# Beginning the stores of normed rows on GpSimd instead of SyncE in a one-core transformer step

## The chip, the cores and the metric

The kernel runs on one core of one Trainium2 chip. Its time is the device time of one execution in microseconds (us), from a run of the whole program; of several runs the median is given. A profile is one further execution with the hardware profiler on. In it the core's engines are PE (TensorE: matmuls), DVE (VectorE), ACT (ScalarE), POOL (GpSimd) and SP (SyncE, which does no arithmetic and here only begins DMAs). Each engine works through its own queue in order, and an instruction that waits for a semaphore holds up whatever stands behind it in that queue.

## What is computed

One layer of a decoder, for a prompt of 2048 tokens and for 64 sampled tokens (8 sequences of 8 tokens with a paged cache of 8192 past positions each). Two groups of heads, one of forgetting attention and one of matrix memory (mLSTM), share an input projection and an output projection. What bears on the change is the block behind them:

```python
def _layer_norm(x, g, b):
    mu = jnp.mean(x, -1, keepdims=True)
    var = jnp.mean(jnp.square(x - mu), -1, keepdims=True)
    return (x - mu) * lax.rsqrt(var + LN_EPS) * g + b

def _block_out(x, fox_h, m_h, ...):
    mix = jnp.concatenate([fox_h, mn], axis=-1) @ w_o      # output projection, 1024 x 1024
    x1 = _layer_norm(DN_ALPHA * x + mix, ln1_g, ln1_b)
    hid = jnp.square(jax.nn.relu(x1 @ w1))                 # MLP, 1024 -> 4096 -> 1024
    return _layer_norm(DN_ALPHA * x1 + hid @ w2, ln2_g, ln2_b)
```

Everything is float32. A product of two float32 matrices is made of three matmuls on high and low halves (`mm3`: lines 157, 158 and 159), and the halves are split by ACT (`split_hi`, line 149) and DVE or GpSimd (`split_lo`, line 152).

## The kernel before, in words

The prompt's 2048 rows are 16 tiles of 128 rows. The kernel goes through stages: the input projection and the matrix memory, the prompt's attention, then the output projection (`phase_o`) and the MLP (`phase_c`). The attention of the sampled tokens runs beside all of them in small steps (`sample_attention`, paced by `tick`): each step gathers pieces of the paged cache by indirect DMAs that GpSimd begins (lines 1671 for keys, 1788 for values), transposes the keys on DVE (1677), and does small products on PE (1700, 1812, 1769) between those of the stage. It ends during the MLP.

**Output projection.** For each tile t, `mix` (SP, line 1299) loads the mixed heads into a landing tile `xr`, of which there are two, and splits them: the high half on ACT, the low half `ml` on GpSimd (L152). `begin` (SP, line 1328) loads the tile's input row into `y`, one of five row buffers that go round. `unit` makes 24 matmuls for each half of the columns and adds them to the row on DVE (1335). `end` norms the row and stores it to a scratch tensor `dx1` in HBM (line 1340). For tiles 2 to 13 the program says, in this order, mix of tile t+1, begin, both units, end; the first and last tiles are written out by hand.

**MLP.** The tiles go in four blocks of four, the last with the 64 sampled rows as a fifth. In a block, `hidden(fc)` and `output(fc)` alternate over 16 slices of the hidden width. Weights come by SP (line 1255) into four buffers `wr`, which the two vectors of the norm share (145), and are split by ACT and DVE. The first output of a block loads the rows `y` from `dx1` by ACT (line 1471), into the same five row buffers; later ones add to them on DVE (1489). Before the last output of a block, `load` brings the next block's rows in for PE (line 1272 on SP, line 1284 on PE). The last output norms each row and stores it to the result (line 1497). The last tile of all, tile 15, has a norm of its own (`last_norm`), which stores its two halves by SP and ACT (line 194).

**The norm** (`layer_norm`, lines 162 to 177) goes over four engines: DVE takes the statistics (170, 171, 172), GpSimd the power -1/2 (173), DVE a product (174), ACT applies scale and bias (175), DVE multiplies by g (176), and GpSimd adds b (177). The store that follows thus waits for GpSimd. In `last_norm` the power on GpSimd is line 188; DVE's last step, line 193, needs it.

**What sets the order.** A planner orders the instructions of each engine from the program's dependences before the program is built, so what stands in the source behind something need not stand there in the queue. The built program begins to differ between the two kernels with the first moved store. A buffer's next writer waits until all readers of the last content are done; for a row that was stored, until the store has landed. Every DMA that one engine's path begins counts on one of eight semaphores in turn, and waits for the one that used it before.

Of the kernel before, what the change touches and what calls it, by code (L numbers as in the profile page):

```python
# [52 lines left out]
def body(ctx, tc, I, O, stages):  # L53
    nc = tc.nc
    V, A, G, T, SY = nc.vector, nc.scalar, nc.gpsimd, nc.tensor, nc.sync
# [17 lines left out]
    dx1 = drm.tile([TOT, D], F32, name="dx1")  # L73
# [69 lines left out]
    def bcast(src, off, n, name, pool=cst, **kw):  # L143
        t = pool.tile([128, n], F32, name=name, **kw)
        SY.dma_start(t, dap(src, off, [[0, 128], [1, n]]))
        return t

    def split_hi(dst, src, scale=1.0):
        last["ACT"] = A.activation(dst, src, AF.Copy, scale=scale)  # L149

    def split_lo(dst, src, hi, eng=None):
        r = (eng or V).tensor_tensor(dst, src, hi.bitcast(F32), op=OP.subtract)  # L152
        if eng is None:
            last["DVE"] = r
# [1082 lines left out]
    def landing(n=128):  # L1237

        return pcw.tile([128, 1024], F32, name="xr", bufs=2)[:n]

    def half_wo(hf, q):

        r = raw().rearrange("p (k c) -> p k c", k=2)
        SY.dma_start(r, I["w_o"][0, q * 256:(q + 1) * 256, hf * 512:(hf + 1) * 512].rearrange("(k p) c -> p k c", p=128))
        return r
# [17 lines left out]
    def row():  # L1263
        return C["py"].tile([128, D], F32, name="y", bufs=5)
# [24 lines left out]
    def phase_o(halves):  # L1289
        C["py"] = es_c.enter_context(tc.tile_pool(name="py", bufs=1, side="right", reuse_waits="tile"))  # L1290
        C["pc"] = pc = es_c.enter_context(tc.tile_pool(name="pc", bufs=1, reuse_waits="tile"))
        es, es_b, es_x = ExitStack(), ExitStack(), ExitStack()
        po_ = es.enter_context(tc.tile_pool(name="po", bufs=1, reuse_waits="tile"))
        pob = es_b.enter_context(tc.tile_pool(name="pob", bufs=1, side="right", reuse_waits="tile"))
        ppo = es.enter_context(tc.tile_pool(name="ppo", bufs=1, space=PSUM, reuse_waits="tile"))

        def mix(t, eng):
            mr = landing().rearrange("p (k c) -> p k c", k=8)
            SY.dma_start(mr, dmv[:, :, t * 128:(t + 1) * 128])
            mh = po_.tile([128, 8, 128], F32R, name="mh", bufs=2)  # L1300
            ml = po_.tile([128, 8, 128], F32R, name="ml", bufs=2)
            split_hi(mh, mr)
            split_lo(ml, mr, mh, eng)
            return mh, ml

        vx["more"] = lambda: pob.tile([128, 1024], F32, name="vx", bufs=2)
        wh, wl = [[], []], [[], []]

        def weights(hf):
            for q in range(4):  # L1310
                r = halves.pop(0) if halves else half_wo(hf, q)
                if hf == 0:
                    h, l = piece(None, r)
                    if q == 0:
                        V.memset(pc.tile([128, 512], F32, name="hq", bufs=1)[:, 0:1], 0.0)
                else:
                    h = pob.tile([128, 2, 512], F32R, name="woh", bufs=4)
                    l = pob.tile([128, 2, 512], F32R, name="wol", bufs=4)
                    split_hi(h, r)
                    split_lo(l, r, h)  # L1320
                wh[hf] += [h[:, 0], h[:, 1]]
                wl[hf] += [l[:, 0], l[:, 1]]

        m, xs = {}, {}

        def begin(t):
            xs[t] = row()
            SY.dma_start(xs[t], x_of(t))

        def unit(t, hf):  # L1330
            s = slice(hf * 512, (hf + 1) * 512)
            ps = ppo.tile([128, 512], F32, name="pw", bufs=4)
            for k in range(8):
                mm3(ps, m[t][0][:, k], m[t][1][:, k], wh[hf][k], wl[hf][k], k == 0, k == 7)
            V.scalar_tensor_tensor(xs[t][:, s], xs[t][:, s], ALPHA, ps, op0=OP.mult, op1=OP.add)
            tick(5.1)

        def end(t):
            layer_norm(xs[t], 128, *gb, pc, "1")
            SY.dma_start(dx1[t * 128:(t + 1) * 128], xs[t])  # L1340

        m[0] = mix(0, None)
        weights(0)
        m[1] = mix(1, None)
        begin(0)
        begin(1)
        unit(0, 0)
        weights(1)
        unit(1, 0)
        gb = [bcast(I[f"ln1_{x}"], 0, D, f"{x}1", pcw, tag="wr", bufs=4) for x in "gb"]  # L1350
        unit(0, 1)
        m[2] = mix(2, G)
        end(0)
        unit(1, 1)
        end(1)
        for t in range(2, 14):
            if t == 13:
                vx["more"] = None
            m[t + 1] = mix(t + 1, G)
            begin(t)  # L1360
            unit(t, 0)
            unit(t, 1)
            end(t)

        m[15] = mix(15, G)
        begin(14)
        begin(15)
        nx = [x1_load(0), x1_load(1)]
        unit(14, 1)
        take_back()  # L1370
        unit(15, 1)
        es_b.close()
        C["px"] = es_c.enter_context(tc.tile_pool(name="px", bufs=1, side="right", reuse_waits="tile"))
        ppx = es_x.enter_context(tc.tile_pool(name="ppx", bufs=1, space=PSUM, side="right", reuse_waits="tile"))
        px_of = lambda: ppx.tile([128, 4, 128], F32, name="px", bufs=2)
        x1_turn(0, 0, nx[0], px_of)
        nx.append(x1_load(2))
        unit(14, 0)
        x1_turn(1, 1, nx[1], px_of)
        nx.append(x1_load(3))  # L1380
        end(14)
        unit(15, 0)
        x1_turn(2, 2, nx[2], px_of)
        x1_turn(3, 3, nx[3], px_of)
        C["w1"] = w1_pieces(0)
        end(15)
        es_x.close()
        es.close()


    def phase_c():
# [38 lines left out]
        for ci, blk in enumerate(CB):  # L1430
# [3 lines left out]
            ys = {}  # L1434
# [25 lines left out]
            def output(fcs):  # L1460
                w2p = [piece(w2[fc * 256 + k * 128:fc * 256 + k * 128 + 128].rearrange("(k p) c -> p k c", p=128)) for fc in fcs for k in range(2)]
                h = [x for fc in fcs for x in H.pop(fc)]
                if 15 in fcs:
                    gb = vecs(2)
                for t in (blk[-1:] + blk[:-1] if 15 in fcs and ci == 3 else blk):
                    n = tok_n(t)
                    s = slice(off[t], off[t] + n)
                    if 0 in fcs:
                        ys[t] = row()
                        with tc.issue_after(last["ACT"].ins):  # L1470
                            A.dma_start(ys[t][:n], dx1[tok_r(t):tok_r(t) + n])
                        if t == 16:
                            V.memset(ys[t][64:128], 0.0)
                    for hf in range(2):
                        cs = slice(hf * 512, (hf + 1) * 512)
                        ps = ppc.tile([128, 512], F32, name="py", bufs=3)
                        for k in range(len(h)):
                            wh, wl = (x[:, 0, cs] for x in w2p[k])
                            if t == 16:
                                mm2(ps, h[k][2], wh, wl, k == 0, k == len(h) - 1)  # L1480
                            else:
                                mm3(ps, h[k][0][:, s], h[k][1][:, s], wh, wl, k == 0, k == len(h) - 1)
                        y = ys[t][:, cs]
                        if 15 in fcs and t == 15 and hf == 1:
                            last_norm(ys[t], n, *gb, pc, ps, O["y_prompt"][0, t * 128:(t + 1) * 128])
                        elif 0 in fcs:
                            V.scalar_tensor_tensor(y, y, ALPHA, ps, op0=OP.mult, op1=OP.add)
                        else:
                            V.tensor_tensor(y, y, ps, op=OP.add)  # L1489
                        tick(1.28 * len(fcs))  # L1490
                    if 15 in fcs and t == 16:
                        lo = landing(64)
                        A.copy(lo, ys[t][64:128])
                        V.tensor_tensor(ys[t][:64], ys[t][:64], lo, op=OP.add)
                    if 15 in fcs and (t, ci) != (15, 3):
                        layer_norm(ys[t][:n], n, *gb, pc, "2")
                        SY.dma_start(O["y_sample"].rearrange("b t d -> (b t) d") if t == 16 else O["y_prompt"][0, t * 128:(t + 1) * 128], ys[t][:n])

            for fc in range(16):
                if fc == 14:  # L1500
# [436 lines left out]
```

## Time and profile before

| what | us |
|---|---|
| median of three runs | 3315.42 |
| lowest and highest run | 3301.81 and 3319.17 |
| the profiled execution | 3323.93 |
| its span, first to last instruction | 3322.2 |
| first and last store of L1340 begun | 1392.9 and 1588.4 |
| first and last store of L1497 begun | 2009.5 and 3312.5 |

A row of instructions in a timeline has the start in us, the time it took, the engine, the line of the kernel, the operation, and what it writes and reads. In brackets stands how long the engine was idle before it and what ended that. A line with groups has the count behind an x, then the busy time and the mean of one in ns, then the idle time before them by what ended it. A row of waits reads: engine and line, then the engine (or DMA) and line it waited for, total us, times, longest. SPq and ACTq are the queues' own instructions: for a DMA they show when it was begun, not when its data landed.

### The profile page before, as it was taken

What the parts mean: (1) busy time and instruction counts of PE and PEld (TensorE: products, weight loads), DVE (VectorE), ACT (ScalarE), POOL (GpSimd) and SP (SyncE); (2) the same over time, 40 slices, a digit from 0 to 9 for tenths busy, and PEclk for the clock granted to TensorE, in tenths of its full rate; (3) what the DMA queues carried; (4) which work ended last, traced back from release to release, by engine and by line L of the source; (5) the groups of instructions that cost most, each with busy time, mean ns of one, the idle gap of its engine ahead of it and who ended that gap; (6) DMA issues with size and microseconds to landing.
All of it is one profiled execution on the core that took longest, in us unless ns stands there. A gap on an engine that the chain in (4) does not pass through costs nothing. (4 is left out here: it accounts for less than half of the span.)

```text
span 3322.2 us, 57307 instructions
## 1 busy us (share of the span) xinstructions
PE 3208.5 (97%) x21420; PEld 2637.1 (79%) x21420; DVE 2121.7 (64%) x5161; ACT 1357.2 (41%) x2670; POOL 931.2 (28%) x1060
## 2 busy tenths in 40 slices
PE   9999999999999999899999999999999999999997
PEld 8998797787877777677777777777767777889997
DVE  6857667566577877556566667656676545755555
ACT  4444244344377777313332333232333333433332
POOL 0112122323254443475333224332242210100001
PEclk9999999999999999999999999999999999999999
DMA  5665766877642233787777678767677554532221
GB/s 172 167 191 177 224 211 190 283 238 226 211 123 86 77 88 108 251 292 254 271 263 259 239 246 304 260 224 273 215 266 258 198 181 142 165 124 86 87 82 67
DMA packets 427294, 646.22 MB, mean 195 GB/s; under 512 B 83149, under 2 KB 320017, under 8 KB 426121
## 3 DMA queue, kind: packets, MB, share of 16 engines
q1 hardware_dynamic: 350184, 363.09, 36.1%
q0 software_dynamic: 74304, 270.57, 22.3%
q10 hardware_dynamic: 2528, 8.91, 0.7%
q8 instruction: 169, 2.77, 0.3%
q14 instruction: 109, 0.89, 0.1%
HBM read 589.63 MB, written 52.83 MB: 193 GB/s over the span
## 5 line engine op out<-in xcount | busy, mean ns | idle before, releaser
L1677 DVE STREAM_TRANSPOSE kT<-kT 128x512 f32<-128x512 f32 x512 | 331.8, 686 | 273.1 <-DMA kT<-cache_k,idxK 272.4
L149 ACT ACTIVATE wh<-wr 128x1024 fp32r<-128x1024 f32 x268 | 278.6, 1056 | 517.7 <-PE py L159 295.1
L1489 DVE TENSOR_TENSOR y<-y,py 128x512 f32<-128x512 f32 x475 | 319.0, 679 | 245.0 <-PE py L159 230.4
L1671 POOL DMA_INDIRECT kT<-cache_k,idxK x256 | 267.3, 1044 | 715.1 <-PE sQ L1700 626.3
L157 PE MATMUL ph<-x1h,wh 128*128 128x512 f32 (+1 forms) x1280 | 455.9, 356 | 8.8 <-ACT wh L149 7.3
L159 PE MATMUL ph<-x1h,wl 128*128 128x512 f32 (+1 forms) x1280 | 452.4, 355 | 4.2 <-DVE wl L152 4.1
L158 PE MATMUL ph<-x1l,wh 128*128 128x512 f32 (+1 forms) x1280 | 453.7, 355 | 0.0
L157 PE MATMUL py<-wh,h 128*128 128x512 f32 x1024 | 402.7, 396 | 3.5 <-DVE y L1489 3.1
L152 DVE TENSOR_TENSOR wl<-wr,wh 128x1024 fp32r<-128x1024 f32 x268 | 333.4, 1249 | 106.1 <-PE ph L159 40.7
L159 PE MATMUL py<-wh,h 128*128 128x512 f32 x1024 | 401.2, 393 | 0.0
L158 PE MATMUL py<-wl,h 128*128 128x512 f32 x1024 | 401.1, 392 | 0.0
L157 PE MATMUL pm<-whi,xhT 128*128 128x256 f32 (+2 forms) x1040 | 302.7, 291 | 3.1 <-ACT acb L542 2.1
L158 PE MATMUL pm<-wlo,xhT 128*128 128x256 f32 (+2 forms) x1040 | 297.6, 286 | 0.0
L159 PE MATMUL pm<-whi,xlT 128*128 128x256 f32 (+2 forms) x1040 | 296.8, 285 | 0.7 <-DVE xlT L152 0.7
L157 PEld LDWEIGHTS ph<-x1h,wh 128*128 128x128 f32 x1280 | 242.2, 189 | 45.8 <-ACT wh L149 8.0
L159 PEld LDWEIGHTS ph<-x1h,wl 128*128 128x128 f32 x1280 | 242.3, 189 | 39.8 <-DVE wl L152 5.4
L158 PEld LDWEIGHTS ph<-x1l,wh 128*128 128x128 f32 x1280 | 242.5, 189 | 33.7 <-issue 2.0
L1788 POOL DMA_INDIRECT vt<-cache_v,idxV x156 | 162.8, 1044 | 316.1 <-PE sO L1812 261.5
L157 PEld LDWEIGHTS py<-wh,h 128*128 128x128 f32 x1024 | 192.4, 188 | 50.7 <-DVE y L1489 6.1
L159 PEld LDWEIGHTS py<-wh,h 128*128 128x128 f32 x1024 | 192.2, 188 | 42.7 <-issue 2.9
L158 PEld LDWEIGHTS py<-wl,h 128*128 128x128 f32 x1024 | 192.4, 188 | 39.9 <-issue 4.1
L157 PEld LDWEIGHTS pm<-whi,xhT 128*128 128x128 f32 (+1 forms) x1040 | 198.4, 191 | 10.4 <-issue 5.3
(420 smaller groups left out, 6623.0 us busy)
## 6 DMA issues: line engine op xcount, KB each, us to landing
wr<-w SPq DMA_DIRECT2D x256, 512.0 KB
wra<-w_in SPq DMA_DIRECT2D x112, 512.0 KB
Rb<-dR SPq DMA_DIRECT2D x128, 128.0 KB
wr<-w_o SPq DMA_DIRECT2D x16, 512.0 KB
xr<-dmix SPq DMA_DIRECT2D x16, 512.0 KB
y<-x_prompt SPq DMA_DIRECT2D x16, 512.0 KB
dx<-y SPq DMA_DIRECT2D x16, 512.0 KB
xr<-dx SPq DMA_DIRECT2D x16, 512.0 KB
```

Source lines behind the costliest of these rows:

```text
L149: last["ACT"] = A.activation(dst, src, AF.Copy, scale=scale)
L152: r = (eng or V).tensor_tensor(dst, src, hi.bitcast(F32), op=OP.subtract)
L157: T.matmul(ps, wh, xh, start=first, stop=False)
L158: T.matmul(ps, wh, xl, start=False, stop=False)
L159: last["PE"] = T.matmul(ps, wl, xh, start=False, stop=stop)
L1489: V.tensor_tensor(y, y, ps, op=OP.add)
L1671: G.indirect_dma_start(out=piece(n), out_offset=None, in_=ck, in_offset=IO(ap=idxK[:, b, j // 2, j % 2:j % 2 + 1], axis=0))
L1677: V.transpose(x, x)
L1788: vx["last"] = G.indirect_dma_start(out=vt.rearrange("p f c -> p (f c)"), out_offset=None, in_=cv, in_offset=IO(ap=idxV[:, b, (kt % 4) * 4 ...
```

## The change

Two lines: the stores that follow `layer_norm` in the output projection (16, one for each tile) and in the MLP (16: fifteen tiles of the prompt and the sampled rows) are begun on GpSimd's queue, where the norm's last sum runs, and no more on SP's.

```diff
         def end(t):
             layer_norm(xs[t], 128, *gb, pc, "1")
-            SY.dma_start(dx1[t * 128:(t + 1) * 128], xs[t])
+            G.dma_start(dx1[t * 128:(t + 1) * 128], xs[t])
...
                     if 15 in fcs and (t, ci) != (15, 3):
                         layer_norm(ys[t][:n], n, *gb, pc, "2")
-                        SY.dma_start(O["y_sample"].rearrange("b t d -> (b t) d") if t == 16 else O["y_prompt"][0, t * 128:(t + 1) * 128], ys[t][:n])
+                        G.dma_start(O["y_sample"].rearrange("b t d -> (b t) d") if t == 16 else O["y_prompt"][0, t * 128:(t + 1) * 128], ys[t][:n])
```

The sampled rows' first norm (`sampled`), which stores to `dx1` too, and `last_norm` stay as they were. The arithmetic is the same. The order in which the planner sets the instructions of all engines changes from the first moved store on: in GpSimd's queue 32 transfers come in, in SP's 32 go, and on PE, DVE and ACT the same instructions stand in a partly different order.

## The prediction, made before the changed kernel ran

> **What bounds the kernel now.** I read the page first, then the busy time by stretches, the waits of the queues, and the timelines around the stores that move.
>
> ```profile
> span 3322.2 us, 57307 instructions
> ...
> PE 3208.5 (97%) x21420; PEld 2637.1 (79%) x21420; DVE 2121.7 (64%) x5161; ACT 1357.2 (41%) x2670; POOL 931.2 (28%) x1060
> ```
>
> TensorE (PE) is busy for 97% of the span; what its idle time leaves is 3322.2 - 3208.5 = 114 us. The view of stretches shows how much of that lies where the moved stores are (first column the stretch, second its length, third PE busy; after the brackets of DVE and ACT comes POOL, which is GpSimd).
>
> ```profile
> core 0: us, PE busy (x) PEld busy (x) DVE busy (x) ACT busy (x) POOL busy (x), PEclk, DMA share, GB/s
> ...
> 1392.00:1540.00 148.00, 144.73 (x918) 112.26 (x916) 80.62 (x200) 34.30 (x57) 101.31 (x82) 1.00 0.82 285
> 1540.00:1590.00 50.00, 43.92 (x285) 33.01 (x284) 32.40 (x68) 15.26 (x24) 29.67 (x21) 0.90 0.74 245
> ...
> 1980.00:2060.00 80.00, 73.99 (x477) 56.11 (x476) 55.47 (x110) 25.71 (x37) 40.46 (x34) 0.98 0.83 296
> ...
> 2420.00:2500.00 80.00, 73.27 (x448) 55.72 (x441) 58.10 (x111) 30.46 (x44) 40.11 (x32) 0.98 0.80 289
> ...
> 2860.00:2940.00 80.00, 77.39 (x447) 68.39 (x446) 51.52 (x79) 34.22 (x56) 11.90 (x8) 0.98 0.52 165
> ...
> 3306.00:3322.00 16.00, 0.00 (x0) 0.00 (x0) 8.89 (x11) 0.37 (x1) 5.64 (x3) 0.57 0.24 98
> ```
>
> The first two rows are the output projection from its first store on, the next three the ends of MLP blocks 0, 1 and 2, the last the tail after the last matmul. PE idles in them, tail aside, for 3.27 + 6.08 + 6.01 + 6.73 + 2.61 = 24.7 us. That is all that a better fed PE could win near these stores. The tail has no PE at all: there every delay counts in full.
>
> **The change part by part.** *What leaves SyncE (SP).* 16 stores of L1340 and 16 of L1497 leave its queue. They stood there as waiters:
>
> ```profile
> SPq L1497 <- POOL y L177: 89.8, 10, 24.7
> ...
> SPq L1340 <- POOL y L177: 83.5, 15, 11.1
> ...
> SPq L1328 <- DMA dx<-y: 20.4, 9, 3.8
> ```
>
> For 89.8 + 83.5 = 173 us SP stood at a store whose sum (L177, on GpSimd) was not done, with loads behind it. This looks large, but 173 us of a queue's standing is no time of PE. What PE waited for says how much of it arrived:
>
> ```profile
> PE sO L1812 <- DMA vt<-cache_v,idxV: 10.2, 7, 2.2
> PE ph L157 <- ACT wh L149: 7.3, 2, 5.0
> PE sO L1812 <- DMA xr<-cache_v,idxV: 6.8, 5, 3.4
> PE px L1284 <- DMA xr<-dx: 4.9, 2, 2.6
> ```
>
> The first and third are gathers that GpSimd itself begins; the second lies at 2500 to 2860, away from the stores. Only the fourth hangs on an SP load near moved stores: two waits, 4.9 us, at the ends of blocks 0 and 1. In SP's order both loads stand ahead of that block's first store, so they win nothing:
>
> ```profile
> 1988.45 0.54 SPq L1272 DMA_DIRECT2D xr<-dx  x1
> 2009.53 0.36 SPq L1497 DMA_DIRECT2D y_prompt<-y  x1
> ...
> 2432.80 6.50 SPq L1272 DMA_DIRECT2D xr<-dx  x2
> 2455.98 0.34 SPq L1497 DMA_DIRECT2D y_prompt<-y  x1
> ```
>
> Bounds of this part: 0 and -24.7 us (all PE idleness above); I take -1 us, near the rows.
>
> *What GpSimd gets.* 32 starts of plain transfers, which this trace never shows on GpSimd. The nearest row is its own gather of as many bytes (512 KB, 128 rows of 4 KB), and against it SP's start of the same store:
>
> ```profile
> L1671 POOL DMA_INDIRECT kT<-cache_k,idxK x256: 932/946/2037, 184.7 to 2575.4; - x128
> ...
> DMA to landing us min/median/max: 4.2/8.2/16.3
> L1340 SPq DMA_DIRECT2D dx<-y x16: 319/326/729, 1392.9 to 1588.4; - x16
> ```
>
> A start is bounded by 0.32 us (if it costs no more than on SP) and 2.04 us (the slowest gather); I take the median, 0.95 us, plus 0.25 us, the gap ahead of a gather in GpSimd's rows below (5.2 us over 20): 1.2 us. 32 x 1.2 = 38 us of GpSimd. Its densest stretch is the projection:
>
> ```profile
> L177 POOL TENSOR_TENSOR y<-y,b 128x1024 f32<-128x1024 f32 x12 | 28.7, 2397 | 23.0 <-DVE y L176 23.0
> L152 POOL TENSOR_TENSOR ml<-xr,mh 128x1024 fp32r<-128x1024 f32 x11 | 26.4, 2398 | 1.2 <-ACT mh L149 1.1
> L1671 POOL DMA_INDIRECT kT<-cache_k,idxK x20 | 19.1, 955 | 5.4 <-issue 5.2 <-PE sO L1812 0.2
> L1788 POOL DMA_INDIRECT vt<-cache_v,idxV x12 | 11.3, 942 | 3.5 <-issue 2.9 <-PE pw L158 0.3 <-PE pw L159 0.3
> L1788 POOL DMA_INDIRECT vx<-cache_v,idxV x10 | 10.3, 1034 | 2.9 <-issue 2.4 <-PE pw L159 0.3 <-PE pw L158 0.2
> ```
>
> In 1392 to 1540 there are 42 gathers with some 5.2 + 2.9 + 2.4 = 10.5 us of gaps between them, so GpSimd is taken for 101.3 + 10.5 = 112 of 148 us. Twelve stores at 1.2 us make it 126, or 85%. Its work has room (L177 alone waited 23.0 us for DVE there), but a single gather, split (L152) or power (L173) is put back by 1.2 us where a store stands ahead. Behind each stand: the gathers (PE's attention products), L152 (the next tile's low half), L173 (DVE's L174 waits for it, and PSUM sums behind that on DVE). The cover is the early start of each: the split for tile t+1 is made a tile ahead, some 148/11 = 13.5 us, against 1.2 us. I take +2.5 us over the whole kernel, about two of 32 reaching PE; if the cover were gone, it would be 38 us.
>
> *What is later.* In the built program a store seldom stands right behind its sum: for 9 of 32 it does, for the others one to seven GpSimd instructions come between, gathers and splits. And the transfer runs in GpSimd's own queue, behind gathers. How long it takes to land is not shown; on SP it was short:
>
> ```profile
> 1414.03 0.32 SPq L1340 DMA_DIRECT2D dx<-y  x1
> 1414.40 1.20 SPq L1684 DMA_DIRECT2D Rb<-dR  x2
> 1416.94 0.34 SPq L1328 DMA_DIRECT2D y<-x_prompt  x1
> ```
>
> The load at 1416.94 goes into the row that the store of 1414.03 frees, so that took at most 2.9 us. From GpSimd I bound the landing by 2.9 and 16.3 us and take the gathers' median, 8.2, since the bytes are the same and the queue too. So a row comes free about 1.2 + 8.2 - 2.9 = 6.5 us later. The waiters are L1328 (eleven rows reused in the projection, on SP) and L1471 (on ACT, at the block ends). Five rows go round, and about three are in use at once (one summed, one normed, one stored), so L1328 asks for its row some two tiles (an estimate, 27 us) before the tile needs it. That hides 6.5 us; I count 0.
>
> *The tail*, where nothing hides:
>
> ```profile
> 3305.28 1.23 DVE L176 TENSOR_TENSOR y<-y,g 128x1024 f32<-128x1024 f32 x1 [0.49 <-ACT y L175]
> ...
> 3307.61 2.40 DVE L176 TENSOR_TENSOR y<-y,g 128x1024 f32<-128x1024 f32 x1
> ...
> 3306.58 2.34 POOL L177 TENSOR_TENSOR y<-y,b 128x1024 f32<-128x1024 f32 x1 [2.04 <-DVE y L176]
> 3310.09 2.34 POOL L177 TENSOR_TENSOR y<-y,b 128x1024 f32<-128x1024 f32 x1 [1.16 <-DVE y L176]
> 3312.39 1.00 POOL L188 TENSOR_TENSOR ln<-ln,nhalf 128x1 f32<-128x1 f32 x1
> ...
> 3314.99 0.36 ACTq L194 DMA_DIRECT2D y_prompt<-y  x1
> ```
>
> GpSimd's last power, L188, starts as soon as the sum of tile 14 ends; DVE's L193 and the last stores wait for it. The built program puts the store of tile 13 between them: +1.2 us for the end. The store of tile 14 comes after L188: 3313.4 + 1.2 + 1.2 = 3315.8, landing by 3320.0 (4.2 us) to 3324.0 (8.2 us), where the span now ends at 3322.2. So the tail costs between 1.2 and 1.8 us; with the vector engine's last steps standing in another order I take +2.
>
> **The sum.** -1 + 2.5 + 0 + 2 = +3.5 us. The profiled execution took 3323.9 us (span 3322.2 and 1.7 around it), so 3327.4 of its kind; it lies 8.5 us above the median of the three runs, 3315.4. I predict 3315.4 + 3.5 = **3319 us**. This is "no change": 0.5% (16.6 us) is about what a measurement of this kernel can tell from none.
>
> **The rivals.** *Faster: SP was what fed PE late.* If all 24.7 us of idleness went, with the tail's +2: 3315.4 - 22.7 = 3293 us. For it speak the 173 us of waiting; against it the four waits of PE above. At the ends of blocks the loads of weights also wait for buffers, which the change doesn't free.
>
> *Slower: the held row.* One mechanism: L1328 stands in SP's queue until the old row's store has landed, and in the built program five of the eleven have the next tile's load (L1299) right behind them. Price 6.5 us each; it decides when the next tile's splits are no longer a tile ahead, so that the 13.5 us of cover are spent. 5 x 6.5 + 2 = +34.5: 3350 us. For it: the stretch at 1392 already moves data at 0.82 of its DMA engines, so stores behind gathers land late; against it: L1328 comes two tiles early.
>
> *Slower: GpSimd before the power.* For the power's result DVE waits little now (waiter, us in total, times):
>
> ```profile
>   DVE ln L174: 24.0, 16
> ```
>
> A store stands one or two places ahead of a power (L173) 14 times; if each held DVE and through it PE, 14 x 1.2 + 2 = +19: 3334 us. The tail shows what could make a start dearer: DVE's L176 takes 1.23 us alone and 2.40 beside GpSimd's L177, so the two hold each other up, and the slowest gather took 2.04 us. At 2.04 + 0.25 us it would be 14 x 2.29 + 2 = +34: 3349 us. It decides when GpSimd is full, 126 going to 148 us in the first stretch. The Trainium skill has the rule for this in "SBUF — State Buffer", in its warning on the "DVE blocks DMA" trap: descriptors of a DMA that GpSimd starts are written by GpSimd, and an operation of DVE that takes the shared port pair locks it out. By that rule the 3349 us would hold if DVE worked so beside every one of these stores; the median gather, at 0.95 us, says that it is rare here.
>
> *It doesn't do what it says:* SP is not freed, because L1328 waits for the store in place of the store waiting for the sum. Then the -1 is 0 and the time 3320 us, not to be told from the forecast.
>
> **How the numbers follow.** Forecast 0.50 and the last rival 0.12, together 0.62 within 0.5%; faster 0.10; held row 0.13 and GpSimd 0.15, together 0.28 slower. The likeliest case's own range is 3302 to 3331. The whole range takes in the faster case nearly to its end and both slower ones: 3297 to 3350 us, which leaves out some 0.1 above and 0.07 below.
>
> **What would show it.** Right: SP's waits on L177 are gone and L1328 waits longer for stores; 32 starts on GpSimd of 0.9 to 1.3 us; PE idle in the five stretches within a few us of 24.7; the last matmul at about the same time and an end some 2 us later behind it. Wrong: PE waits on pw for mh or ml (the held row); DVE's L174 waiting for L173 well above 24.0 us (GpSimd is full); starts of 2 us (the lock); or PE's idle time near the stores halved (faster).

## The result and the profile after

The changed kernel took 3330.37 us in the median, the kernel before 3317.15 us in runs beside it: a ratio of 1.0038, with a 95% interval from 1.0025 to 1.0050. That is 8 to 17 us more, within the 0.5% that was called "no change", but above zero, and about 9 us more than the sum of +3.5 us. The profiled execution took 3333.75 us, its span 3332.0 us, 9.8 us more than before. The page of the changed kernel begins:

```profile
span 3332.0 us, 57310 instructions
...
PE 3210.1 (96%) x21420; PEld 2638.7 (79%) x21420; DVE 2128.2 (64%) x5161; ACT 1356.9 (41%) x2670; POOL 941.0 (28%) x1092
```

PE does the same work (3210.1 us against 3208.5), GpSimd has 32 instructions more. The time went into idleness of PE, and the view of stretches says where:

```profile
1392.00:1540.00 148.00, 136.32 (x867) 104.36 (x867) 75.97 (x185) 32.56 (x53) 102.19 (x88) 0.98 0.75 256
1540.00:1590.00 50.00, 41.82 (x256) 32.28 (x257) 31.72 (x69) 12.06 (x20) 27.53 (x24) 0.93 0.73 258
...
1980.00:2060.00 80.00, 73.77 (x467) 57.49 (x469) 59.04 (x103) 31.03 (x47) 34.24 (x30) 1.00 0.80 280
...
2420.00:2500.00 80.00, 74.59 (x486) 56.46 (x486) 57.74 (x107) 27.04 (x38) 41.95 (x36) 1.00 0.71 256
...
2860.00:2940.00 80.00, 78.95 (x451) 69.30 (x450) 54.82 (x83) 38.86 (x61) 14.22 (x12) 1.00 0.55 187
```

Idle near the stores is now 11.7 + 8.2 + 6.2 + 5.4 + 1.1 = 32.6 us instead of 24.7. The first row alone has 8.4 us more, against 7.9 us for all five together. (A second pair of profiles, h3 and h4 below, has 24.1 and 32.9 us in the five rows.) Counted by matmuls, so that a shift does not blur it: from the 10,000th matmul to the 11,500th it took 252.5 us before and 265.7 us after. I call this **the stretch**. Ahead of it the two kernels are within 5 us of each other, and 0.6 us apart where it begins; behind it the changed one stays 3 to 18 us late, and 11.1 us at the last matmul. What one profile shows behind the stretch proves little: h2's below ends its matmuls 11.0 us later than h3's, by delays in the MLP, and its median time is no longer.

SyncE got what the change gives. Of its waits, those of L1340 and L1497 for the sum are gone, and this is what L1328 shows, over the whole span:

```profile
SPq L1328 <- DMA dx<-y: 67.5, 11, 18.5
```

So 173 us of waiting left SyncE, 47 us came in at L1328, and PE won nothing. What PE met in the stretch is above all one wait. PE's timeline (start, duration, then in brackets the idle time ahead):

```profile
1515.04 0.40 PE L158 MATMUL pw<-wol,mh 128*128 128x512 f32 x1
1521.12 0.80 PE L159 MATMUL pw<-wh,ml 128*128 128x512 f32 x1 [5.68 <-POOL ml L152]
1521.71 0.63 PE L157 MATMUL pw<-wh,mh 128*128 128x512 f32 x1
...
1525.12 0.47 PE L159 MATMUL pw<-wh,ml 128*128 128x512 f32 x1
1525.43 0.40 PE L157 MATMUL pw<-wh,mh 128*128 128x512 f32 x1
```

PE stands 5.68 us for `ml` of tile 12 (counted by the tiles' order), and then runs nine matmuls 0.43 us apart, where 0.23 us is usual: 2 us more. In the kernel before the same product came without a wait:

```profile
1512.06 0.39 PE L159 MATMUL pw<-wh,ml 128*128 128x512 f32 x1
```

Why is that split late? GpSimd's timeline before, from the gathers ahead of it to the split:

```profile
1487.52 0.99 POOL L1671 DMA_INDIRECT kT<-cache_k,idxK  x1 [0.18 <-issue]
...
1497.17 0.93 POOL L1671 DMA_INDIRECT kT<-cache_k,idxK  x1 [0.30 <-issue]
1498.12 2.42 POOL L177 TENSOR_TENSOR y<-y,b 128x1024 f32<-128x1024 f32 x1
...
1506.65 0.94 POOL L1659 COPY qb<-qt 32x128 f32<-32x128 f32 x3 [5.88 <-DMA kT<-cache_k,idxK]
...
1508.55 2.40 POOL L152 TENSOR_TENSOR ml<-xr,mh 128x1024 fp32r<-128x1024 f32 x1
```

And of the changed kernel:

```profile
1492.28 0.99 POOL L1671 DMA_INDIRECT kT<-cache_k,idxK  x1 [0.17 <-issue]
...
1501.68 0.94 POOL L1671 DMA_INDIRECT kT<-cache_k,idxK  x1 [0.30 <-issue]
1502.64 0.59 POOL L173 TENSOR_TENSOR ln<-ln,nhalf 128x1 f32<-128x1 f32 x1
...
1513.89 0.94 POOL L1659 COPY qb<-qt 32x128 f32<-32x128 f32 x3 [10.42 <-DMA kT<-cache_k,idxK]
1514.92 2.35 POOL L177 TENSOR_TENSOR y<-y,b 128x1024 f32<-128x1024 f32 x1
...
1518.06 0.61 POOL L1340 DMA_DIRECT2D dx<-y  x1
1518.69 2.37 POOL L152 TENSOR_TENSOR ml<-xr,mh 128x1024 fp32r<-128x1024 f32 x1
```

The split begins 10.1 us later. On GpSimd the planner now has the power of tile 9 behind the gathers (at 1502.64; before it stood ahead of them, as the lists below show), so that tile's sum falls behind the copies to `qb` (2.35 us), and its store with it (0.6 us). The copies wait until the gathers in flight have landed. They end 7.2 us later, because the last gather is begun 4.5 us later (another store, at 1495.75, takes 0.6 us of that) and lands 2.7 us slower (0.7 us in the second pair of profiles).

GpSimd's queue is not the split's only path. The split also reads the high half `mh`, which ACT makes, and that comes 6.0 us later too (the kernel before, then the changed one):

```profile
1507.11 1.04 ACT L149 ACTIVATE mh<-xr 128x1024 fp32r<-128x1024 f32 x1
...
1513.15 1.04 ACT L149 ACTIVATE mh<-xr 128x1024 fp32r<-128x1024 f32 x1
```

In ACT's queue it stands behind the exponentials of the sampled attention (L1737), whose scores hang on the same late gathers. So with the gathers as late as they were, the split could not have begun before 1514.19, whatever stood ahead of it on GpSimd: 6.0 of the 10.1 us come down ACT's path already, as I read the rows from the late gathers, and GpSimd's queue holds the split for another 4.5 us, where it was 0.4 us before.

PE had little cover for this split. In the kernel before it was done at 1510.95, 1.1 us ahead of its first product (0.2 us in h3); the splits of tiles 10, 11 and 13 were done 8.5 to 13.4 us ahead. In the changed kernel PE, 3.4 us late by then, had come to that product at 1515.44, and the split was done at 1521.06: 5.6 us, the wait.

GpSimd's order as built, by tile (m: split L152, s: sum L177, p: power L173, g: gather, S: store, Q: the copies to `qb`, b: L1661):

```
before    s7 m10 p  g x8      s8 m11 p  g x8        s9 Q p b m12
changed   s7 g x2 S7 g x6  m10 p s8 m11 g x3 S8 g x5  p Q s9 p b S9 m12
```

### The profile page after: what moved, and what is told of

It reads as the page before. It is cut to its first block, busy times and chain, and to the rows that moved or that the text cites. A ratio compares the mean times of both kernels' runs of the same rounds, so it can differ in the third digit from the quotient of the medians.

```text
span 3332.0 us, 57310 instructions
## 1 busy us (share of the span) xinstructions
PE 3210.1 (96%) x21420; PEld 2638.7 (79%) x21420; DVE 2128.2 (64%) x5161; ACT 1356.9 (41%) x2670; POOL 941.0 (28%) x1092
## 3 DMA queue, kind: packets, MB, share of 16 engines
q1 hardware_dynamic: 345640, 346.57, 34.7%
## 5 line engine op out<-in xcount | busy, mean ns | idle before, releaser
L1671 POOL DMA_INDIRECT kT<-cache_k,idxK x256 | 261.4, 1021 | 728.3 <-PE sQ L1700 640.2
L152 DVE TENSOR_TENSOR wl<-wr,wh 128x1024 fp32r<-128x1024 f32 x268 | 335.5, 1256 | 108.5 <-PE ph L159 42.0
```

What stands on the lines that cost most here:

```text
L1671: G.indirect_dma_start(out=piece(n), out_offset=None, in_=ck, in_offset=IO(ap=idxK[:, b, j // 2, j % 2:j % 2 + 1], axis=0))
```

## The experiments

Times are compared with the kernel before run beside them; its median was 3357.1 us in the set of e1 to e5, 3375.5 in that of g1 to g3 and e7, and 3314.7 in that of h1 to h4, each set on another chip, so only ratios are set side by side. "Stretch" is the one profile's 10,000th to 11,500th matmul.

| kernel | stores on GpSimd, projection + MLP | ratio, 95% interval | stretch, us |
|---|---|---|---|
| e1_proj | 16 + 0 | 1.0031, 1.0014 to 1.0048 | 266.4 |
| e2_mlp | 0 + 16 | 1.0003, 0.9982 to 1.0023 | 250.1 |
| e3_qb | 16 + 16, copies behind the store | 1.0029, 1.0010 to 1.0048 | 263.9 |
| e5_late | 16 + 16, row load behind the mixed heads | 1.0000, 0.9982 to 1.0017 | 258.4 |
| g1_from4 | 12 + 16 | 1.0014, 0.9997 to 1.0032 | 259.4 |
| g2_one | 1 + 0 | 1.0013, 0.9994 to 1.0031 | 259.9 |
| g3_ml12 | 16 + 16, one split on DVE | 1.0038, 1.0021 to 1.0055 | 270.0 |
| e7_act | none, all 32 on ScalarE | 0.9988, 0.9975 to 1.0002 | 262.4 |
| h3_before | none | (one run, 3313.0 us) | 252.7 |
| h4_after | 16 + 16 | 1.0040, 1.0021 to 1.0059 | 266.7 |
| h1_order | none, order alone | 1.0011, 0.9993 to 1.0030 | 261.4 |
| h2_from8 | 8 + 16 | 0.9998, 0.9980 to 1.0015 | 252.9 |

The stretch is no stand-in for the time: e5's is 8.3 us longer than e2's of the same set, and its time is no longer.

My first theory was the held row: I read the late load L1299 on SyncE, behind an L1328 that stood 18.5 us, as the reason for the late split.

**e1_proj and e2_mlp: which stores.** The kernel before, with only line 1340 (e1) or only line 1497 (e2) changed from `SY` to `G`.

> Only the 16 stores of the projection (L1340) go to GpSimd; those of the MLP (L1497) stay on SyncE. Theory 1 (held row): the whole loss is one episode of the projection near 1500 us, in which the copies to qb (L1659, about 10 us of waiting for DMAs in flight) stand ahead of the sum L177 on GpSimd, the store behind that sum begins late, SyncE's row load L1328 waits for it and the mixed-head load L1299 stands behind it. It expects 10 to 13 us over the kernel before (3327 to 3330 us), TensorE idle about 11 us in 1392 to 1540 us (3.3 before), and TensorE's wait for ml (L152) there. Theory 2 (GpSimd's occupancy: each store costs its engine, wherever it is): half the loss of the change, 5 to 7 us. Theory 3 (the planner's new order costs some us anywhere): anything between -5 and +12, with the idle time elsewhere.

> Only the 16 stores of the MLP's end (L1497) go to GpSimd; those of the projection stay on SyncE. Theory 1 (held row): no loss, -2 to +1 us against the kernel before, since the episode near 1500 us isn't there; the time from the last matmul to the end about 1.3 us shorter (15.4 in place of 16.7 us). Theory 2 (GpSimd's occupancy): half the loss of the change, 5 to 7 us. Theory 3 (the planner's new order): anything from -5 to +8, with TensorE idle at the start of block 1 near 2513 us (5.6 us on y L1487) as its sign.

A loss shows in e1 and none in e2. That speaks against a loss shared by the number of stores (occupancy of GpSimd as such), but each interval still holds half of the loss; h2 below settles it. e1 has GpSimd's order of the changed kernel, e2 that of the kernel before. e2's tail did not shorten (20.1 us from the last matmul to the end).

**e3_qb: the copies.** Their place was my trigger. `kx["sum"]` is the latest store of L1340.

```diff
-        for a in range(4):
-            s = slice(a * 32, a * 32 + 32)
-            G.tensor_copy(qb[s, :, a * 8:a * 8 + 8], z["qt"][s, 0])
+        with tc.issue_after(kx["sum"].ins) if "sum" in kx else ExitStack():
+            for s in [slice(a * 32, a * 32 + 32) for a in range(4)]:
+                G.tensor_copy(qb[s, :, s.start // 4:s.start // 4 + 8], z["qt"][s, 0])
```

> The changed kernel with one order added: the copies to qb (L1659) come behind the latest store of the projection, so the sum and its store are no longer queued behind their wait. Theory 1 (held row, set off by the place of the copies): 9 to 12 us below the changed kernel, -3 to +3 us against the kernel before; SyncE's L1328 waits of 18.5 us gone, TensorE idle 3 to 5 us in 1392 to 1540 us. Theory 2 (GpSimd's occupancy): the time of the changed kernel, 3328 to 3333 us, since all 32 stores stay on GpSimd. Theory 3: within 5 us of the changed kernel on either side, with the idle time moved elsewhere.

A miss: 1.0029, the loss stayed. Its GpSimd shows why:

```profile
1494.49 0.59 POOL L173 TENSOR_TENSOR ln<-ln,nhalf 128x1 f32<-128x1 f32 x1
1501.81 2.39 POOL L177 TENSOR_TENSOR y<-y,b 128x1024 f32<-128x1024 f32 x1 [6.73 <-DVE y L176]
...
1506.94 0.61 POOL L1340 DMA_DIRECT2D dx<-y  x1 [0.28 <-POOL bn L1661]
...
1508.93 3.29 POOL L152 TENSOR_TENSOR ml<-xr,mh 128x1024 fp32r<-128x1024 f32 x1
```

The copies wait for nothing now, but the power still comes at the end of the gathers, the sum waits 6.73 us for DVE's part of the norm, which follows the power, and the split stands behind both. Here the high half was the nearer limit: ACT had it done at 1507.63, only 1.3 us ahead of the split. PE still waits for `ml`, 3.9 us.

**e5_late: the row load.** From tile 5 on, L1328 behind that iteration's L1299, `C["ld"]`.

```diff
-            xs[t] = row()
-            SY.dma_start(xs[t], x_of(t))
+            with tc.issue_after(C["ld"].ins) if t > 4 else ExitStack():
+                xs[t] = row(); SY.dma_start(xs[t], x_of(t))
```

> The changed kernel with another order added: from tile 5 on, the row load L1328 comes behind that iteration's mixed-head load L1299, so that a row still being stored holds one load fewer. The copies to qb stay ahead of the sum. Theory 1 (held row): the link is loosened, so 5 to 11 us of the changed kernel's 13 come back (3319 to 3325 us); TensorE's wait for ml L152 of 5.7 us is gone. If the late sum itself, and not the load behind the row, were what TensorE waits for, nothing comes back. Theory 2 (GpSimd's occupancy): no change against the changed kernel, 3328 to 3333 us. Theory 3: within 5 us of the changed kernel on either side.

All of it came back, which looked like the held row. But the edit moved GpSimd's list too: here it says `Q b p b m12 s9 s10`, the split ahead of the sum. So this run doesn't separate the two. The changed kernel's own SyncE does (L1299 of tile 12 and then of 13 are the first two rows; the last has those of 14 and 15):

```profile
1484.01 0.38 SPq L1299 DMA_DIRECT2D xr<-dmix  x1
...
1493.86 0.38 SPq L1299 DMA_DIRECT2D xr<-dmix  x1
...
1505.78 15.60 SPq L1328 DMA_DIRECT2D y<-x_prompt  x2
1521.46 5.91 SPq L1299 DMA_DIRECT2D xr<-dmix  x2
```

The load for the split that PE waited for was begun at 1484.0, 34.7 us ahead of the split. The load at 1521.46, behind the held rows, could not have begun before 1521.06, when that very split freed its landing tile. The held row was there and held up nothing that PE needed; my first theory fell. The new one is **theory A: the planner's order on GpSimd**.

**g1_from4, g2_one, g3_ml12, e7_act.** The projection's stores by tile (first plus line g1; second g2, with the MLP's stores back on `SY`), all stores on ScalarE (third, e7, with the MLP's on `A` too), or one split on DVE (last, g3, which keeps the changed kernel's stores):

```diff
-            G.dma_start(dx1[t * 128:(t + 1) * 128], xs[t])
+            (SY if 0 <= t <= 3 else G).dma_start(dx1[t * 128:(t + 1) * 128], xs[t])
+            (G if 5 <= t <= 5 else SY).dma_start(dx1[t * 128:(t + 1) * 128], xs[t])
+            A.dma_start(dx1[t * 128:(t + 1) * 128], xs[t])
...
-            m[t + 1] = mix(t + 1, G)
+            m[t + 1] = mix(t + 1, None if t == 11 else G)
```

> The changed kernel with the stores of the projection's tiles 0 to 3 back on SyncE; the other 12 and the MLP's 16 stay on GpSimd. Theory A (GpSimd's order): the planner then puts the power and the sum of tile 9 ahead of the second block of gathers and of the copies to qb, as it did before the change, and the low half ml of tile 12 is no longer queued behind a sum that stands behind the copies; although 28 of 32 stores stay on GpSimd, the loss goes: within -4 to +4 us of the kernel before, TensorE's wait for ml gone, the matmuls near 1520 us without a slow stretch. Theory B (held row: a row load on SyncE waits for the store, and the mixed-head load behind it): the late stores are the same ones, so the loss stays, 9 to 13 us over the kernel before. Theory C (GpSimd's occupancy): 28/32 of the loss, 9 to 12 us.

> The kernel before with one single store, that of tile 5 in the projection, on GpSimd; the other 31 stay on SyncE. Theory A (GpSimd's order): this one store is enough for the planner to put the power and the sum of tile 9 behind the second block of gathers and the copies to qb, with ml of tile 12 behind them: TensorE waits about 4 us for ml (5.7 us less the 0.6 and 0.9 us of the two stores that are not there) and runs at the lower clock for some 4 us behind it, 6 to 11 us over the kernel before. Theory B (held row) and theory C (occupancy): one store in 32 costs at most 1 us, within 2 us of the kernel before.

> The changed kernel, all 32 stores on GpSimd, with the low half ml of tile 12 alone made by VectorE in place of GpSimd. SyncE's order and its waits for rows being stored stay. Theory A (GpSimd's order): TensorE's wait of 5.7 us for that ml goes, and with it the 2 us of slow matmuls behind it: 5 to 9 us below the changed kernel, 3 to 8 us over the kernel before. Theory B (held row): the load behind the held row is what is late, so nothing comes back: 10 to 14 us over the kernel before. Theory C (occupancy): 1 us comes back at most.

> The kernel before with all 32 stores begun by ScalarE, neither by SyncE nor by GpSimd. GpSimd's order is that of the kernel before. SyncE's waits for the sum L177 go, and its row load L1328 waits for a store that comes from another engine, as in the changed kernel. Theory A (GpSimd's order): no loss from GpSimd, so -4 to +4 us against the kernel before, unless ScalarE's own queue makes high halves late, which would show as a wait for mh or PTs. Theory B (held row): 9 to 13 us over the kernel before, since SyncE's row loads then wait for the stores just as in the changed kernel. Theory C (occupancy of GpSimd): no loss.

g1 (order of tile 9 as before, 28 stores on GpSimd) and g2 (order as after, one store) came out at +0.14% and +0.13%, with intervals that hold zero and part of what each theory expects of a loss: by time neither decides. g2's PE does wait for `ml`, 2.2 us (about 4 were expected), with one store on GpSimd, and g1's does not. e7 is clear: no loss, with L1328 waiting for stores 49.0 us in the projection, so longer waits there are harmless to that amount. Its stretch, 262.4 us, is long for a kernel without loss; no profile of the kernel before was taken in that job, where PE also waited on keys (2.9 us on DVE's turned `kT`), so I don't set it against the 252.5 and 252.7 us of the kernel before.

g3 was a miss for A in its simple form: with that split on DVE nothing came back. PE's waits in its projection:

```profile
PE px L1284 <- DVE x1l L152: 8.8, 3, 5.2
PE sO L1812 <- DMA vx<-cache_v,idxV: 3.4, 1, 3.4
PE pw L159 <- DVE ml L152: 1.9, 1, 1.9
```

The wait for `ml` fell to 1.9 us, but the gathers, powers and sums stay as late as they were, and what hangs on them is late next. The one split is where the late list is first felt, not the whole of it.

**h1_order, h2_from8, with both kernels beside them.** The order without the stores, and the stores without the order. In h1 all stores stay on SyncE, and the power of tile 5 alone (`kx["t"]` is the tile being normed) is ordered behind the latest gather of values; from there the planner gives the list of the changed kernel without its stores: `s7 g x8 m10 p s8 m11 g x8 p Q s9 p b m12`. In h2 the stores of tiles 8 to 15 and of the MLP are on GpSimd, and the list is that of before: `m10 p g x8 s8 S8 m11 p g x8 s9 Q S9 p b m12`. The first plus line is h1's, the other h2's.

```diff
-        G.tensor_tensor(rs[:np_, 1:2], rs[:np_, 0:1], nhalf[:np_, 0:1], op=OP.pow)
+        with tc.issue_after(vx["last"].ins) if kx.get("t") == 5 else ExitStack(): G.tensor_tensor(rs[:np_, 1:2], rs[:np_, 0:1], nhalf[:np_, 0:1], op=OP.pow)
...
+            (SY if 0 <= t <= 7 else G).dma_start(dx1[t * 128:(t + 1) * 128], xs[t])
```

> The kernel before, unchanged, for a profile of it taken beside those of the three other kernels. Every theory: a ratio of 1.000; the stretch from the 10000th to the 11500th matmul, which took 252.5 us in the first profile of this kernel, within 4 us of that. If the gathers land later on this chip, that stretch and the MLP are longer here, and the other kernels' stretches are compared with this one.

> The changed kernel, unchanged, beside the kernel before. Theory A (GpSimd's order) and theory B (held row) alike: 1.002 to 1.005 of the kernel before, as measured first, with TensorE's wait of 4 to 7 us for ml of tile 12 near 1520 us and a slow stretch of the clock behind it. If the wait is not there and the time is the same, neither theory holds.

> The kernel before with all 32 stores on SyncE and one order added: the power L173 of tile 5 comes behind the latest gather of values. From there the planner gives GpSimd the list of the changed kernel without its stores: the power and the sum of tile 9 behind the second block of gathers, the sum behind the copies to qb, ml of tile 12 behind that sum. Theory A (GpSimd's order): though nothing is moved to GpSimd, most of the loss appears: 4 to 9 us over the kernel before, TensorE waiting 2 to 5 us for ml near 1515 us. Theory B (held row) and theory C (occupancy by stores): no loss, within 2 us.

> The changed kernel with the stores of the projection's tiles 0 to 7 back on SyncE; tiles 8 to 15, which are those of the stretch where the loss arises, and the MLP's 16 stay on GpSimd. The planner then keeps GpSimd's list of the kernel before, with the stores put in. Theory A (GpSimd's order): no loss, -3 to +3 us against the kernel before, no wait for ml near 1515 us. Theory B (held row) and theory C (occupancy in that stretch): the loss of the changed kernel, 9 to 13 us, as all the stores of the stretch are begun by GpSimd.

The same 130 us in the four profiles, kernel before first, each from its view of stretches:

```profile
1470.00:1600.00 130.00, 123.72 (x825) 93.75 (x818) 77.27 (x183) 39.23 (x67) 78.97 (x66) 0.97 0.80 284
```

The changed kernel:

```profile
1470.00:1600.00 130.00, 113.60 (x705) 86.50 (x704) 70.83 (x169) 34.59 (x59) 80.50 (x73) 0.93 0.74 254
```

h1, the order alone:

```profile
1470.00:1600.00 130.00, 116.80 (x725) 88.94 (x724) 74.78 (x170) 37.05 (x63) 73.77 (x62) 0.95 0.75 266
```

h2, the stores alone:

```profile
1470.00:1600.00 130.00, 121.38 (x768) 92.88 (x767) 76.40 (x172) 39.00 (x66) 81.85 (x74) 0.99 0.82 285
```

PE idles 6.3, 16.4, 13.2 and 8.6 us. And the wait for the split of tile 12, in the changed kernel's PE timeline:

```profile
1518.23 0.79 PE L159 MATMUL pw<-wh,ml 128*128 128x512 f32 x1 [5.69 <-POOL ml L152]
```

in h1's:

```profile
1513.97 0.80 PE L159 MATMUL pw<-wh,ml 128*128 128x512 f32 x1 [4.96 <-POOL ml L152]
```

and in h2's:

```profile
1510.69 0.50 PE L159 MATMUL pw<-wh,ml 128*128 128x512 f32 x1 [0.99 <-POOL ml L152]
```

Nearer to the wait, the 100 matmuls from the 10,700th to the 10,800th, which hold it, took 21.5 and 22.2 us in the two profiles of the kernel before, 32.5 and 30.6 us in those of the changed kernel, 30.6 us in h1 and 23.0 us in h2.

h2 is decisive for the stores: 24 of 32 on GpSimd, among them those of tiles 8 to 15, which stand where the time is lost, cost nothing that shows (0.9980 to 1.0015, below the 1.0021 to 1.0059 of the changed kernel beside it). They do use up the small cover: PE waits 0.99 us. h1 shows the other half: with no store on GpSimd the wait is there, 4.96 us, and the 100 matmuls take as long as in the changed kernel of the same set. Its stretch is 8.7 us longer than h3's, of 14.0 in the changed kernel. Its time says less: 1.0011, -2 to +10 us, which holds 8.7 but also zero. And e5 took 29.0 us for the same 100 matmuls, with no loss in its time. So **shown**: without the changed order the stores cost nothing that shows, and the order alone makes the wait and the delay at it. **Open**: the other 5.3 us of stretch between h1 and the changed kernel, of which 4.2 lie ahead of those 100 matmuls and 1.1 behind (stores standing among a list that is already late would fit, and wasn't tried by itself), and by time alone how much of 13 us the order makes. That a single store's place sets the order off was read from the built lists, not timed apart.

No version beat the kernel before beyond its interval; e7 came nearest, at -0.12% (-0.25 to +0.02).

## Why the prediction held, and the step of it that failed

The time lies in the range and within 0.5%, but the sum was +3.5 us where some +13 were measured. That it still held is owed to the width of the band, and so to luck: what made the 13 us is in no term of the sum. The 3334 us of "GpSimd before the power" are nearer, by another mechanism.

- **SyncE, -1 us.** Right that its 173 us of waiting was no time of PE: e2 and h2 free SyncE of 16 and 24 stores and win nothing.
- **GpSimd, +2.5 us: the step that failed.** The prediction put it as "a single gather, split (L152) or power (L173) is put back by 1.2 us where a store stands ahead", with 13.5 us of cover. The start was over-priced, and both the place and the cover were taken as the same for all:

```profile
L1340 POOL DMA_DIRECT2D dx<-y x16: 571/586/616, 1397.0 to 1602.1; - x16
...
DMA to landing us min/median/max: 2.9/6.0/10.6
```

  A start is 0.59 us, not 0.95, and with the stores alone (h2) the term is 0 within -7 to +5 us. But the working kept every instruction in the place it had and only put stores between. The planner didn't: it moved a power, a sum and a block of gathers, and one split came 10.1 us later, against 0.6 us for a store's start. And the 13.5 us were the mean distance of two splits: the cover of this one was 1.1 us. The built list had been read for what stands behind the stores, not for what else had changed places.
- **A row freed later, 0 us.** Right, though L1328 waits 47 us more: e7 had 29 of them (49.0 us for 20.4) and no loss. The landing took 6.0 us in the median, under the 8.2 assumed.
- **The tail, +2 us: wrong in sign.** From the start of the last matmul to the end it took 17.1 us before and 15.8 after, in both pairs of profiles (e2's 20.1 stands against that). The foreseen delay is there, with the store of tile 13 ahead of L188 and DVE waiting for it:

```profile
3324.48 0.60 POOL L1497 DMA_DIRECT2D y_prompt<-y  x1
3325.10 1.06 POOL L188 TENSOR_TENSOR ln<-ln,nhalf 128x1 f32<-128x1 f32 x1
3326.13 0.57 POOL L1497 DMA_DIRECT2D y_prompt<-y  x1
3326.20 1.42 DVE L193 SCALAR_TENSOR_TENSOR y<-y,ln,b 128x512 f32<-128x512 f32 x2 [0.45 <-POOL ln L188]
...
3327.65 0.36 ACTq L194 DMA_DIRECT2D y_prompt<-y  x1
```

  The last store is begun 11.4 us behind the start of the last matmul, 9.9 before: 1.5 us more, of which the start ahead of L188 is 0.6 and DVE's wait 0.45. But begun at 3327.65 it ends the span at 3332.0, 4.4 us on; before, begun at 3314.99, it took 7.2 us. Why is open: in e2, with the same stores on GpSimd, it took 8.7 us.
- **The signs.** "PE waits on pw for mh or ml" was to show the held row. The wait came, and it was not the held row: that sign named the victim, and the same victim has more than one cause. What decided was that the load behind the held rows was none that this split needed. Of the signs of being right only SyncE's came: a start took 0.59 us and not 0.9 to 1.3, PE idled 32.6 us near the stores, and the last matmul was 11.1 us late.
- **GpSimd before the power.** No start of a store was over 0.63 us in any run, and DVE's wait for L173 was

```profile
DVE ln L174 <- POOL ln L173: 20.6, 15, 3.8
```

  under the 24.0 us of before (28.3 and 28.8 in h2 and g1, without a loss that shows). So the 2.29 us that the rival took did not come. The Trainium skill's rule in "SBUF — State Buffer", on the "DVE blocks DMA" trap, is neither borne out nor refuted here: no run shows a store's start on GpSimd that DVE held up, and none shows whether DVE ever held the port pair beside one. Whether a landing was late for that reason, the traces don't tell.

## What to carry to other kernels

Where a planner sets the order, an added instruction is not priced by its own time: lay the two built lists of the engine side by side, find the places where other instructions changed their order, and price the worst of those against the slack of its consumer. When the wait shows up, ask first when each input of the late instruction was ready: what passed after the last of them is its own engine's queue (here 4.5 us), and what passed before has to be followed up through the engine that made that input. And test order and work apart: one kernel with the order and without the work, one with the work and the old order.

## What the runs showed of the hardware

- A plain store of 512 KB took GpSimd 0.55 to 0.62 us to begin, in every run; a gather of as many bytes took it 0.94 us in the median, and the same store 0.32 to 0.36 us on SyncE and on ScalarE.
- A long wait cost PE more than its length. After 5.68 us of idleness the granted clock was half. The changed kernel in stretches of 4 us (PE busy, granted clock, DMA share, GB/s):

```profile
1512.00:1516.00 4.00, 2.65 (x11) 1.00 0.22 76
1516.00:1520.00 4.00, 0.00 (x0) 0.81 0.20 81
1520.00:1524.00 4.00, 2.88 (x7) 0.50 0.55 188
1524.00:1528.00 4.00, 4.00 (x18) 0.84 0.41 124
```

  It came back 4.0 us after the restart (1521.12 to 1525.12). At 0.23 us each the nine starts in between would have taken 2.1 us, so this wait of 5.7 us cost 7.6. The Trainium skill has the rule in "TensorE: Matmul & The Clock Gate", Part 1: an idle window of about 3.4 us halves the clock, and as long a busy one restores it. The trace agrees, with 5.68 us idle and 4.0 us busy.
